# Weight slices at eight places in SBUF, and another order of the contraction in the second feed-forward

## The chip, the cores and the metric

The kernel runs on one NeuronCore of a Trainium2 chip. The metric is the device time of one launch in microseconds. The kernel before takes 2028.67 us, the median of three runs (2028.02 to 2029.2).

## The reference

One inference step of a one-layer decoder on 288 positions: 256 of a prompt and 8 x 4 of samples that are being decoded. D_MODEL is 2048, D_FF is 5632, and everything is float32.

```python
def rms_norm(x, g):
    ...
def swiglu(x, w_gate, w_up, w_down):
    return (jax.nn.silu(x @ w_gate) * (x @ w_up)) @ w_down

def decoder_layer(x, lp, h0, k_past, v_past):
    x = x + 0.5 * swiglu(rms_norm(x, lp['ffn1_norm']), lp['ffn1_w_gate'], lp['ffn1_w_up'], lp['ffn1_w_down'])
    hn = rms_norm(x, lp['mix_norm'])
    z = hn @ lp['w_in']
    u, q, k, v = jnp.split(z, ...)
    y_ssm, h_last = s5_mixer(u, h0, ...)            # state space scan over the positions
    ...                                             # norms of q and k, keys of the cache
    y_attn = window_attention(q, kk, vv, ...)       # window of 128 positions
    merged = jnp.concatenate([rms_norm(y_ssm, lp['ssm_out_norm']), rms_norm(y_attn, lp['attn_out_norm'])], axis=-1)
    x = x + merged @ lp['w_out']
    x = x + 0.5 * swiglu(rms_norm(x, lp['ffn2_norm']), lp['ffn2_w_gate'], lp['ffn2_w_up'], lp['ffn2_w_down'])
    return x, k_state, v_state, h_last
```

The positions are columns here: the residual x is kept as 16 tiles of 128 features x 288 positions, and every projection has a weight block as the stationary operand and a tile of activations as the moving one.

## The kernel before

**Pieces and splits.** All weights are read once, in 680 pieces of 128 x 1024, 128 x 768 or 128 x 640 float32: gate and up projections, down projections, then w_in and w_out in the mixing stage, then the second feed-forward. The class `Weights` brings them in. `load` (line 75) issues a piece's DMA from SP into a tile `raw`, of which there are five. `split` (line 83) makes two tiles of it for TensorE's fp32r format: `wh`, the rounded weights (a cast on ACT, line 88), and `wl`, what the rounding lost (a subtraction on DVE, line 89). Of `wh` and of `wl` there are three each. `next` (line 103) hands the present piece to TensorE, splits up to two pieces ahead and loads up to five ahead. It also runs other work that is bound to the number of a piece. So each engine's order is written out by hand, and each queue is strictly in that order.

**Matmuls.** Activations are split the same way, into `xh` and `xl` (or `hh` and `hl` for what goes into a down projection). A piece holds eight slices of 128 columns (six or five in a down projection). For each slice k `mm3` issues three matmuls into one PSUM bank, lines 272 to 274: `wh` with the high tile, `wh` with the low tile, `wl` with the high tile. Each streams 128 x 288 and has its own weight load of 128 x 128.

**Places.** A moving tile of 288 float32 takes 1,152 bytes of a partition, four and a half times 256, so the next tile starts 128 bytes beside it, modulo 256. Between the 16 tiles `xh` and the 16 tiles `xl` lies a tile of 32 float32, `gap_x`, that serves nothing else; `gap_r` and `gap_y` do the same for `hh` and `hl`. So the moving operands of a slice's three matmuls, and of neighbouring slices, start in turn 128 bytes beside a multiple of 256 and on one. `gap_w`, 56 float32 ahead of the weight tiles, makes `raw`, `wh` and `wl` start on multiples of 256, and with 512 bytes to a slice every slice does.

**Stages.** The first feed-forward takes pieces 0 to 303, in four rounds of eleven gate and up units and a down projection of 16 x 2 pieces each. The small tables of the state space part are made beside it, and a few transposes on TensorE come between its pieces. The mixing stage takes pieces 304 to 375, and the second feed-forward 376 to 679.

Of the kernel before, what the change touches and what calls it, by code (L numbers as in the profile page):

```python
# [10 lines left out]
F32 = mybir.dt.float32  # L11
F32R = mybir.dt.float32r
# [5 lines left out]
P = 128  # L18
# [7 lines left out]
N = T * W1  # L26
# [4 lines left out]
HALF = 8 * P  # L31
# [15 lines left out]
class Weights:  # L47
# [28 lines left out]
    def load(self):  # L76
        ap = self.pieces[self.nl]
        n = ap.shape[-1]
        t = self.pool.tile([P, HALF], F32, name="raw", bufs=5)
        self.nc.sync.dma_start(t[:, :n], ap)  # L80
        self.raw[self.nl] = (t, n)
        self.nl += 1

    def split(self):
        t, n = self.raw.pop(self.ns)
        wh = self.pool.tile([P, HALF], F32R, name="wh", bufs=3)
        wl = self.pool.tile([P, HALF], F32R, name="wl", bufs=3)
        self.nc.scalar.copy(wh[:, :n], t[:, :n])  # L88
        self.nc.vector.tensor_tensor(wl[:, :n], t[:, :n], wh[:, :n].bitcast(F32), op=ALU.subtract)  # L89
        self.hl[self.ns] = (wh, wl)  # L90
        self.ns += 1
# [25 lines left out]
def tile_hymba_step(ctx, tc, io):  # L117
# [14 lines left out]
    def ffn_units(l):  # L132
        seq = []
        for c in range(NCK):
            for f in range(CH):
                if not (c > 0 and f == 0):
                    seq.append(("gu", c * CH + f))
            if c + 1 < NCK:
                seq.append(("gu", (c + 1) * CH))
            seq.append(("down", c))  # L140
        return seq
# [27 lines left out]
    xh = [cp.tile([P, N], F32R, name="xh%d" % k) for k in range(KT)]  # L169
    cp.tile([P, 32], F32, name="gap_x")  # L170
    xl = [cp.tile([P, N], F32R, name="xl%d" % k) for k in range(KT)]
# [96 lines left out]
    def mm3(ps, wh, wl, kts, rh, rl, first, last):  # L268
        n = len(kts)
        for a, k in enumerate(kts):  # L270
            s = slice(a * P, (a + 1) * P)
            pe.matmul(ps, wh[:, s], rh[k], start=first and a == 0, stop=False)  # L272
            pe.matmul(ps, wh[:, s], rl[k], start=False, stop=False)  # L273
            pe.matmul(ps, wl[:, s], rh[k], start=False, stop=last and a == n - 1)  # L274

    def projs(n):

        ps = [pm.tile([P, 512], F32, name="main") for _ in range(n)]
        for hf in range(2):
            for p_ in ps:  # L280
                wh, wl = W.next()
                mm3(p_[:, :N], wh, wl, range(8 * hf, 8 * hf + 8), xh, xl, hf == 0, hf == 1)
        return ps

    def proj():
        return projs(1)[0]

    def ffn(l, post, hp, first):
        HH, HL = {}, {}
        hold = Hold(W.i + first)  # L290
        early = [] if l else projs(3)

        def gate(f, pg, s2):
            t1 = tp.tile([P, N], F32, name="t1")
            s1 = tp.tile([P, N], F32, name="s1")
            dve.tensor_tensor(t1, pg[:, :N], R, op=ALU.mult)  # L296
            act.activation(s1, t1, AF.Silu)  # L297
            pool_e.tensor_tensor(s2, s1, R, op=ALU.mult)  # L298

        def up(f, pu, s2):  # L300
            h = tp.tile([P, N], F32, name="h")
            hh = hp.tile([P, N], F32R, name="hh")
            if f == 0:
                hp.tile([P, 32], F32, name="gap_r", bufs=1)
            hl = hp.tile([P, N], F32R, name="hl")
            dve.tensor_tensor(h, pu[:, :N], s2, op=ALU.mult)  # L306
            act.copy(hh, h)  # L307
            dve.tensor_tensor(hl, h, hh.bitcast(F32), op=ALU.subtract)  # L308
            HH[f % CH, f // CH], HL[f % CH, f // CH] = hh, hl

        def gu(f):
            s2 = tp.tile([P, N], F32, name="s2")
            pg = early.pop(0) if early else proj()
            hold(lambda: gate(f, pg, s2))
            pu = early.pop(0) if early else proj()
            hold(lambda: up(f, pu, s2))

        def down(c):
            rh = {k: HH.pop((k, c)) for k in range(CH)}
            rl = {k: HL.pop((k, c)) for k in range(CH)}  # L320
            for d in range(KT):
                ps = pm.tile([P, 512], F32, name="main")
                wh, wl = W.next()
                mm3(ps[:, :N], wh, wl, range(6), rh, rl, True, False)
                wh, wl = W.next()
                mm3(ps[:, :N], wh, wl, range(6, CH), rh, rl, False, True)
                dve.scalar_tensor_tensor(x[d], ps[:, :N], 0.5, x[d], op0=ALU.mult, op1=ALU.add)  # L327
                if c == NCK - 1:
                    post(d)

        for kind, j in ffn_units(l):
            (gu if kind == "gu" else down)(j)
# [275 lines left out]
    with ExitStack() as es:  # L608
        mix(tc, nc, io, es, W, MIX0, dict(
            x=x, xh=xh, xl=xl, gains=gains, ident=ident, ones=ones, acc=acc, R=R, tp=tp,  # L610
            dr=dr, pm=pm, pa=pa, proj=proj, mm3=mm3, norm=norm, rsqrt=rsqrt, now=now, Hold=Hold,
            mats=mats, e4=e4, h4=h4, h0=h0, post=post_norm(32)))
# [646 lines left out]
```

## Time and profile before

| | |
|---|---|
| median of three runs | 2028.67 us |
| profiled execution, its own time | 2031.1 us |
| span from first to last instruction | 2029.3 us |
| mean granted TensorE clock | 0.997 |
| TensorE matmuls, share of the span | 99% (15,248) |
| DVE, ACT, POOL | 60%, 42%, 15% |
| moved by DMA | 359.04 MB, 177 GB/s |

Busy time of TensorE counts from a matmul's start to its modelled end, and matmuls overlap in it. It tells that the engine had work, not how fast the work went. That is read from how many matmuls start in a stretch. PEld is the engine's weight load, which runs beside the matmuls.

### The profile page before, as it was taken

The page shows a single profiled execution, that of the slowest core. Times are in us where ns is not written, and L with a number is a line of the kernel's source. Part 1 is how long each engine was busy: PE and PEld are TensorE (multiplying, and loading weights), DVE is VectorE, ACT ScalarE, POOL GpSimd, SP SyncE. Part 2 cuts the span into 40 slices and gives each one's busy share as a digit, 9 for nine tenths or more (in the row PEclk, how much of TensorE's full clock was granted, in tenths as well). Part 3 has the DMA queues.
Part 4 walks back from the last instruction along what each step waited for, and adds up shares of the span by engine and source line. Part 5 has one row for each costly group of instructions (what it writes and reads, how often), then busy time and mean ns, then how long its engine had stood idle before and what let it go on. Part 6 is the DMA issues. An engine that isn't in the chain of part 4 may idle for free. (4 is left out here: it accounts for less than half of the span.)

```text
span 2029.3 us, 37632 instructions
## 1 busy us (share of the span) xinstructions
PE 2008.7 (99%) x15248; PEld 1995.9 (98%) x15248; DVE 1212.0 (60%) x1873; ACT 851.5 (42%) x1334; POOL 295.8 (15%) x451
## 2 busy tenths in 40 slices
PE   8999999999999999999999999999999999999999
PEld 7999999999999999999989999999999999999999
DVE  5577666666656645686787874455444544454444
ACT  5433443444444434533476543333333333333332
POOL 3110011001110000212367730000000000000000
PEclk9999999999999999999999999999999999999999
DMA  6555645565656565678634445556555655465554
GB/s 225 194 164 148 210 158 203 173 208 162 203 172 196 176 197 151 216 235 276 221 120 136 151 162 166 164 144 190 161 164 147 185 165 163 147 181 168 166 159 148
DMA packets 122622, 359.04 MB, mean 177 GB/s; under 512 B 22448, under 2 KB 30256, under 8 KB 121264
## 3 DMA queue, kind: packets, MB, share of 16 engines
q1 hardware_dynamic: 114672, 340.81, 53.4%
q10 hardware_dynamic: 7776, 15.83, 2.3%
q8 instruction: 119, 1.95, 0.4%
q14 instruction: 55, 0.45, 0.1%
HBM read 338.40 MB, written 20.22 MB: 177 GB/s over the span
## 5 line engine op out<-in xcount | busy, mean ns | idle before, releaser
L89 DVE TENSOR_TENSOR wl<-raw,wh 128x1024 fp32r<-128x1024 f32 (+2 forms) x680 | 760.2, 1118 | 540.0 <-ACT wh L88 538.1
L272 PE MATMUL main<-xh,wh 128*128 128x288 f32 x3136 | 932.6, 297 | 6.1 <-ACT xh L180 6.1
L273 PE MATMUL main<-xl,wh 128*128 128x288 f32 x3136 | 927.4, 296 | 1.3 <-DVE xl L181 1.3
L274 PE MATMUL main<-xh,wl 128*128 128x288 f32 x3136 | 927.5, 296 | 0.9 <-DVE wl L89 0.7
L88 ACT CAST wh<-raw 128x1024 fp32r<-128x1024 f32 (+2 forms) x680 | 643.5, 947 | 626.8 <-PE main L273 413.1
L272 PEld LDWEIGHTS main<-xh,wh 128*128 128x128 f32 x3136 | 593.6, 189 | 7.1 <-ACT xh L180 6.1
L273 PEld LDWEIGHTS main<-xl,wh 128*128 128x128 f32 x3136 | 593.6, 189 | 2.4 <-DVE xl L181 2.1
L274 PEld LDWEIGHTS main<-xh,wl 128*128 128x128 f32 x3136 | 593.4, 189 | 1.3 <-DVE wl L89 1.3
L272 PE MATMUL main<-hh,wh 128*128 128x288 f32 x1664 | 494.1, 297 | 0.0
L273 PE MATMUL main<-hl,wh 128*128 128x288 f32 x1664 | 491.1, 295 | 0.3 <-DVE hl L674 0.3
L274 PE MATMUL main<-hh,wl 128*128 128x288 f32 x1664 | 490.6, 295 | 0.0
L273 PEld LDWEIGHTS main<-hl,wh 128*128 128x128 f32 x1664 | 313.8, 189 | 0.7 <-DVE hl L674 0.5
L274 PEld LDWEIGHTS main<-hh,wl 128*128 128x128 f32 x1664 | 313.7, 189 | 0.0
L272 PEld LDWEIGHTS main<-hh,wh 128*128 128x128 f32 x1664 | 313.2, 188 | 0.4
L298 POOL TENSOR_TENSOR s<-s,R 128x288 f32<-128x288 f32 x88 | 71.2, 809 | 1255.2 <-ACT s L297 1255.2
L297 ACT ACTIVATE s<-t 128x288 f32<-128x288 f32 x88 | 39.1, 445 | 238.3 <-DVE t L296 238.3
L307 ACT CAST hh<-h 128x288 fp32r<-128x288 f32 x88 | 38.1, 433 | 240.1 <-DVE h L306 240.1
L327 DVE SCALAR_TENSOR_TENSOR x<-main,x 128x288 f32<-128x288 f32 x128 | 58.4, 456 | 50.9 <-PE main L274 49.0
L306 DVE TENSOR_TENSOR h<-main,s 128x288 f32<-128x288 f32 x88 | 40.2, 457 | 77.3 <-PE main L274 77.1
L296 DVE TENSOR_TENSOR t<-main,R 128x288 f32<-128x288 f32 x88 | 40.2, 457 | 64.5 <-PE main L274 64.0
L308 DVE TENSOR_TENSOR hl<-h,hh 128x288 fp32r<-128x288 f32 x88 | 40.3, 458 | 44.0 <-ACT hh L307 44.0
L190 POOL TENSOR_TENSOR acc<-acc,sq 128x288 f32<-128x288 f32 x45 | 48.9, 1086 | 56.5 <-ACT sq L186 55.2
(263 smaller groups left out, 877.9 us busy)
## 6 DMA issues: line engine op xcount, KB each, us to landing
raw<-in_w_gu SPq DMA_DIRECT2D x352, 512.0 KB, 3.5
raw<-in_w_dn SPq DMA_DIRECT2D x128, 384.0 KB, 3.1
raw<-in_w_dn SPq DMA_DIRECT2D x128, 320.0 KB, 2.9
raw<-in_w_in SPq DMA_DIRECT2D x40, 512.0 KB, 4.1
raw<-in_w_out SPq DMA_DIRECT2D x32, 512.0 KB, 3.4
mats<-stage ACTq DMA_DIRECT2D x8, 1536.0 KB, 7.0
mb<-mats SPq DMA_DIRECT2D x8, 768.0 KB, 5.1
ma<-mats SPq DMA_DIRECT2D x8, 512.0 KB, 4.2
```

The costliest lines, as they stand in the source:

```text
L88: self.nc.scalar.copy(wh[:, :n], t[:, :n])
L89: self.nc.vector.tensor_tensor(wl[:, :n], t[:, :n], wh[:, :n].bitcast(F32), op=ALU.subtract)
L190: eng.tensor_tensor(acc, acc, sq, op=ALU.add)
L272: pe.matmul(ps, wh[:, s], rh[k], start=first and a == 0, stop=False)
L273: pe.matmul(ps, wh[:, s], rl[k], start=False, stop=False)
L274: pe.matmul(ps, wl[:, s], rh[k], start=False, stop=last and a == n - 1)
L296: dve.tensor_tensor(t1, pg[:, :N], R, op=ALU.mult)
L297: act.activation(s1, t1, AF.Silu)
L298: pool_e.tensor_tensor(s2, s1, R, op=ALU.mult)
L306: dve.tensor_tensor(h, pu[:, :N], s2, op=ALU.mult)
L308: dve.tensor_tensor(hl, h, hh.bitcast(F32), op=ALU.subtract)
L327: dve.scalar_tensor_tensor(x[d], ps[:, :N], 0.5, x[d], op0=ALU.mult, op1=ALU.add)
```

## The change

It has three parts. `wh` and `wl` become tiles of 1,088 columns, of which 1,024 are used, from column o on. o is 0 for the first eight pieces, 8 for the next eight, and so on to 56, and then 0 again: 0, 32, 64 ... 224 bytes beside a multiple of 256. There are four `raw` tiles in place of five. And in the gate and up projections of the second feed-forward (l = 1, so step = 2) the eight slices of a piece are taken in the order 0 2 4 6 1 3 5 7. A slice keeps its columns in the piece, b in `mm3`.

```diff
     def load(self):
...
-        t = self.pool.tile([P, HALF], F32, name="raw", bufs=5)
+        t = self.pool.tile([P, HALF], F32, name="raw", bufs=4)
...
     def split(self):
         t, n = self.raw.pop(self.ns)
-        wh = self.pool.tile([P, HALF], F32R, name="wh", bufs=3)
-        wl = self.pool.tile([P, HALF], F32R, name="wl", bufs=3)
+        o = 8 * (self.ns // 8 % 8)
+        wh = self.pool.tile([P, HALF + 64], F32R, name="wh", bufs=3)[:, o:o + HALF]
+        wl = self.pool.tile([P, HALF + 64], F32R, name="wl", bufs=3)[:, o:o + HALF]
...
         for a, k in enumerate(kts):
-            s = slice(a * P, (a + 1) * P)
+            b = k - kts[0]
+            s = slice(b * P, (b + 1) * P)
...
-    def projs(n):
+    def projs(n, step=1):
...
-                mm3(p_[:, :N], wh, wl, range(8 * hf, 8 * hf + 8), xh, xl, hf == 0, hf == 1)
+                ks = [8 * hf + a for b in range(step) for a in range(b, 8, step)]
+                mm3(p_[:, :N], wh, wl, ks, xh, xl, hf == 0, hf == 1)
...
-    def proj():
-        return projs(1)[0]
+    def proj(step=1):
+        return projs(1, step)[0]
...
-            pg = early.pop(0) if early else proj()
+            pg = early.pop(0) if early else proj(1 + l)
...
-            pu = early.pop(0) if early else proj()
+            pu = early.pop(0) if early else proj(1 + l)
```

The number and the kinds of instructions on every engine are the same, and no row on ACT, DVE, POOL or SP changes its place. Lines move down by one to three (`mm3`'s are 274 to 276 after). The places in SBUF of all tiles but `raw`, `wh` and `wl` are the same modulo 512. In the built program 3,744 of the 14,400 matmuls of `mm3` have weights 0 or 128 bytes beside a multiple of 256, and 10,656 have them at one of the six other places.

TensorE's order changes in the second feed-forward alone. Its first gate piece begins so before; xh_87 to xh_94 are the high tiles of slices 0 to 7, xl_104 to xl_111 the low ones, and even slices have their high tile 128 bytes beside a multiple of 256 and their low tile on one:

```order
8265 L272 MATMUL main<-xh_87,wh 128x288
8266 L273 MATMUL main<-xl_104,wh 128x288
8267 L274 MATMUL main<-xh_87,wl 128x288
8268 L272 MATMUL main<-xh_88,wh 128x288
8269 L273 MATMUL main<-xl_105,wh 128x288
8270 L274 MATMUL main<-xh_88,wl 128x288
8271 L272 MATMUL main<-xh_89,wh 128x288
```

And after, in the same place:

```order
8265 L274 MATMUL main<-xh_87,wh 128x288
8266 L275 MATMUL main<-xl_104,wh 128x288
8267 L276 MATMUL main<-xh_87,wl 128x288
8268 L274 MATMUL main<-xh_89,wh 128x288
8269 L275 MATMUL main<-xl_106,wh 128x288
8270 L276 MATMUL main<-xh_89,wl 128x288
8271 L274 MATMUL main<-xh_91,wh 128x288
```

Slice 0 is followed by slice 2, so two high tiles of even slices stand next to each other (rows 8267 and 8268) where a high tile of an odd slice stood.

The end of that piece and the begin of the next on TensorE, before; xh_95 is the first high tile of the second half of the features:

```order
8283 L272 MATMUL main<-xh_93,wh 128x288
8284 L273 MATMUL main<-xl_110,wh 128x288
8285 L274 MATMUL main<-xh_93,wl 128x288
8286 L272 MATMUL main<-xh_94,wh 128x288
8287 L273 MATMUL main<-xl_111,wh 128x288
8288 L274 MATMUL main<-xh_94,wl 128x288
8289 L272 MATMUL main<-xh_95,wh 128x288
```

And after:

```order
8283 L274 MATMUL main<-xh_92,wh 128x288
8284 L275 MATMUL main<-xl_109,wh 128x288
8285 L276 MATMUL main<-xh_92,wl 128x288
8286 L274 MATMUL main<-xh_94,wh 128x288
8287 L275 MATMUL main<-xl_111,wh 128x288
8288 L276 MATMUL main<-xh_94,wl 128x288
8289 L274 MATMUL main<-xh_95,wh 128x288
```

The piece ends with slices 5 and 7, whose neighbours are again of one class (rows 8285 and 8286), and the step to the next piece, from slice 7 to slice 8, is as before.

## The prediction

> **What bounds the kernel now.** I read the page first: its busy shares, and the shares of the chain that ended last.
>
> ```profile
> PE 2008.7 (99%) x15248; PEld 1995.9 (98%) x15248; DVE 1212.0 (60%) x1873; ACT 851.5 (42%) x1334; POOL 295.8 (15%) x451
> PEclk9999999999999999999999999999999999999999
> PE 41%; DVE 0%; issue 0%
> PE main L272 14%; PE main L274 14%; PE main L273 14%; PE main L206 0%; DVE x L327 0%
> ```
>
> TensorE is busy in 99% of the span at full clock, and the chain, as far back as it is followed (41% of the span), is nothing but the three matmul lines. So the end is set by how far apart the matmuls start. There are 14,400 of them in these lines (3 x 3136 + 3 x 1664), and 1 ns more in each spacing is 14.4 us of the kernel. The duration that a group shows for one matmul (some 296 ns) is of no use here, since two or three are drawn over each other; the spacing has to be counted. The next view does that: the busy time of TensorE in chosen stretches, with the count x of matmuls. Each is drawn 0.29 us long, so about two of a count were already running when the stretch opened; I leave those two off.
>
> ```profile
> core 0: us, PE busy (x), PEclk, DMA share, GB/s
> 46.00:168.00 122.00, 122.00 (x917) 1.00 0.52 168
> 294.00:355.00 61.00, 61.00 (x471) 1.00 0.56 189
> 370.00:382.00 12.00, 12.00 (x94) 1.00 0.41 112
> 495.00:556.00 61.00, 61.00 (x472) 1.00 0.59 190
> 571.00:598.00 27.00, 27.00 (x210) 1.00 0.56 185
> 695.00:794.00 99.00, 99.00 (x764) 1.00 0.54 174
> 1192.00:1335.00 143.00, 143.00 (x1075) 1.00 0.50 159
> 1547.00:1616.00 69.00, 69.00 (x522) 1.00 0.59 174
> ...
> 913.20:916.30 3.10, 3.10 (x15) 0.50 1.03 425
> ```
>
> The reader is to see three speeds of the same instruction at the same clock. From 46 to 168 us it is 122/915 = 133.3 ns, and from 1192 to 1335 us 143/1073 = 133.3. From 294 to 355 us it is 61/469 = 130.1, and from 695 to 794 us 99/762 = 129.9. In a down projection (1547 to 1616 us) it is 69/520 = 132.7. The last row is a stretch in which half the clock was granted: 3.10/13 = 238 ns, so one matmul alone needs about 119 ns at full clock. The other 11 to 14 ns are not its own streaming. The timeline of a 130 ns stretch shows what they are tied to:
>
> ```profile
> 320.07 0.29 PE L274 MATMUL main<-xh,wl 128*128 128x288 f32 x1
> 320.07 0.19 PEld L272 LDWEIGHTS main<-xh,wh 128*128 128x128 f32 x1
> 320.20 0.29 PE L272 MATMUL main<-xh,wh 128*128 128x288 f32 x1
> 320.20 0.19 PEld L273 LDWEIGHTS main<-xl,wh 128*128 128x128 f32 x1
> 320.33 0.29 PE L273 MATMUL main<-xl,wh 128*128 128x288 f32 x1
> ```
>
> The load for the next matmul starts when a matmul starts, and the next matmul follows 0.13 us later, although streaming takes only 0.12. So I read the spacing as the time of a weight load. The chain of waits in a 133.3 ns stretch gives each spacing as the length of a piece:
>
> ```profile
> 1190.82 0.14 PE main L274
> 1190.96 0.13 PE main L272
> 1191.09 0.13 PE main L273
> 1191.22 0.13 PE main L274
> 1191.36 0.14 PE main L272
> ...
> 1191.89 0.14 PE main L273
> ```
>
> One spacing in four is long: 0.14 us, at 1190.82, 1191.36 and 1191.89. With three at 131 the fourth is 4 x 133.3 - 3 x 131 = 140 ns. A tile that is streamed has 1,152 bytes, four and a half times 256, and by the gap of 128 bytes between the high and the low tiles each matmul's operand lies 128 bytes away, modulo 256, from the operand before it. Four steps keep the class, so the long spacing always falls on the same one of the two classes. By the addresses in the built program it is the class that lies 128 bytes beside a multiple of 256; the other starts on the multiple, as every weight slice does. So equal matmuls differ by where operand and weights stand to each other, and half of the shifted class pays. In the 130 ns stretches nobody pays.
>
> **The change part by part.** *Places of the weights.* Nothing is added on any engine: the same 680 ACT casts and 680 DVE subtractions write the same sizes, and the 14,400 matmuls read the same sizes. What changes is the first byte. Counted in the built program, 3,744 matmuls get slices 0 or 128 bytes beside a multiple of 256, and 10,656 get 32, 64, 96, 160, 192 or 224. At 0 nothing changes; 128 only swaps which class of operand is the shifted one, and I price both at nothing. For the other six places there is no row, since no stretch has them. Bounds from the nearest rows: not under the 130.0 of the fast stretches, not over the 140 of the long spacing. What do they pay now? The five fast stretches are 260 us, or 2,000 matmuls; 4,224 are in the down projections at 132.7; 8,176 remain at 133.3. The mean is 132.7. So the bounds are (130.0 - 132.7) x 10,656 = -29 us and (140 - 132.7) x 10,656 = +78 us. Between them I take 134.4. At these six places both classes of operand stand off the weights, as only one does now. If each class pays as the shifted class pays today, the spacing is the mean of 140 and 131, 135.5. If a paid collision also spares the next three matmuls, whichever class they are, it stays 133.3, and only the fast stretches are lost. 134.4 lies half way. That is 1.7 x 10,656 = +18 us.
>
> *Order 0 2 4 6 1 3 5 7.* It adds no instruction. In 176 pieces of the second feed-forward (4,224 matmuls, at 133.3 now) operands of one class meet six times in a piece (the third matmul of one slice and the first of the next). Before, such a meeting is found only in the down projections, once in 33 matmuls (eleven slices), and there the mean is 132.7: a meeting is worth 33 x 0.6 = 20 ns. Six of them cannot bring a piece under 130.0, so the gain is at most 3.3 x 4,224 = 14 us. The loss is bounded by the half of a piece in which two matmuls in three are of the shifted class: (2 x 135.5 + 131)/3 = 134.0, or 0.7 x 4,224 = +3 us. Only a quarter of these pieces keep a place at which I know the pattern, so I take a quarter of 14: -4 us.
>
> *Four raw buffers for five.* The load five pieces ahead now waits for the split of the piece one ahead, not of the present one: one piece later, 3.2 us (24 x 133 ns). Queued behind it on SP are the other loads of the mixing stage, and the matmuls there wait for those.
>
> ```profile
> raw<-in_w_gu SPq DMA_DIRECT2D x352, 512.0 KB, 3.5
> raw<-in_w_dn SPq DMA_DIRECT2D x128, 384.0 KB, 3.1
> SPq L80 <- DVE wl L89: 1402.7, 577, 7.3
> ACT wh L88 <- PE main L273: 413.1, 272, 6.7
> ACT wh L88 <- DMA raw<-in_w_gu: 5.4, 4, 2.5
> 865.00:1136.00 271.00, 263.44 (x2135) 0.99 0.60 192
> ```
>
> SP already waits 577 times for a split, and ACT, which splits, waits for TensorE 272 times but for a landing 4 times, 5.4 us in all. A raw piece has about four pieces' time from its issue to its use, 8.8 us where pieces are shortest (16.5 matmuls, 2.2 us each), against 3.1 us to land and some 2 for the splits. That cover hides the later issue. If it is gone, each late landing holds TensorE. The one stretch with idle time on TensorE, the mixing stage, has 271 - 263.4 = 7.6 us of it; I bound the cost by as much again, +8, and below by 0, since a later issue lets nothing start earlier. I take +1.
>
> *The sum.* This execution took 2031.1 us, 2029.3 of it the span. 2031.1 + 18 - 4 + 1 = 2046. The median of the runs is 2028.67, 2.4 below it, so I forecast 2044, with 2033 to 2062 as this case's own range (133.3 to 135.5 elsewhere). Under 0.2%, 4 us, a measurement cannot tell from no change.
>
> **The rivals.** *The other places are fast* (other side). A collision then needs slice and operand exactly 128 bytes apart, and at six of eight places every matmul runs at 130.0 as from 695 to 794 us. That is -29 - 4, or 1996. The point that decides is a mean of 132.7 at the new places. For it: the fast stretches show that 130.0 is held for 99 us. Against it: it is the weaker pattern, 2,000 matmuls of 14,400, and from 1192 to 1335 us, between the same operands, it is not met.
>
> *Weights' place is indifferent*, and the long spacing comes from something else. Then only the order is left, 2025 to 2029. The Trainium skill says this: TensorE: Matmul & The Clock Gate, section "Step-by-step: what each phase is for", has two independent read ports, so that loading the next weights takes nothing from the running matmul. SBUF — State Buffer, section "Who interferes with whom", has TensorE never waiting on anyone. Against this rival stands 133.3 beside 130.0 at clock 1.00, with one class of operand marked; for it, that the trace never shows another place of the weights, so the cause may sit in the operand's place alone.
>
> *Every load at a 32-byte place is long.* If slices at 32, 96, 160 and 224 (7,104 matmuls) need more reads, each spacing is 140: 7.3 x 7,104 = +52, about 2078 with the rest as forecast or better; all six places would give 2107.
>
> *Late loads.* If landings in the mixing stage come late one after the other, TensorE waits in that stage twice as long as now: +8 in place of +1, and about 2051. It decides where a landing takes over four pieces' time.
>
> **How the numbers follow.** The chances go by how much of the trace each has on its side. Forecast 0.43; fast places 0.26; indifferent 0.13; long loads 0.14; late loads 0.04. Faster is 0.26 and a third of the indifferent, 0.30. No change is the rest of it and 0.05 from the forecast's lower edge, 0.14. Slower is 0.56. The range 1999 to 2084 leaves out the faster part of the fast places and the worse part of the long loads, about 0.1 each. Cases of both signs hold the chance, so the forecast's own range above is the narrower statement.
>
> **What the profile after would show.** Groups of eight pieces are 25 us long, so stretches cut at their bounds give the spacing of each place: 133.3 or less at 0 and 128, 133.3 to 135.5 at the others if I am right; 130.0 there makes me wrong, and so does 140 in every second group. In the second feed-forward the groups at 0 and 128 should show less than 133.3. ACT should still wait for landings some 5 us in all, and the mixing stage should keep its 7.6 us of idle TensorE. What I can least exclude is that a step of the place every 25 us itself throws the matmuls from one pattern into the other.

## The result, and the profile after

The changed kernel takes 2039.26 us, the median of four runs (2038.23 to 2042.96), against 2028.35 for the kernel before: a ratio of 1.0057, 95% interval 1.004 to 1.0075, 11 us slower. The profiled execution of after took 2038.27 us, its span 2036.5, 7.2 more than the span before. The two profiled executions lie closer together than the medians: that of before, 2031.1 us, is longer than the four timed ones (2027.44 to 2029.2), that of after is among the shorter of its four.

Lines of the page of after, on busy shares, clock and the chain that ended last:

```profile
PE 2011.7 (99%) x15248; PEld 1998.6 (98%) x15248; DVE 1213.6 (60%) x1873; ACT 852.3 (42%) x1334; POOL 295.8 (15%) x451
PEclk9999999999999999999999999999999999999999
PE 41%; DVE 0%; issue 0%
```

Nothing here tells the two kernels apart: TensorE is busy in 99% of the span at full clock, as before. The difference is in how far apart the matmuls start, and in one stage. The busy time of TensorE in the three stages, first feed-forward, mixing stage, second feed-forward, before (cut at the first matmul of the next stage):

```profile
0.00:864.70 864.70, 855.26 (x6435) 1.00 0.58 186
864.70:1181.40 316.70, 309.14 (x2478) 0.99 0.58 188
1181.40:2029.30 847.90, 844.26 (x6339) 1.00 0.53 163
```

And after:

```profile
0.00:871.00 871.00, 860.70 (x6435) 1.00 0.57 184
871.00:1190.80 319.80, 308.98 (x2479) 0.99 0.59 187
1190.80:2036.50 845.70, 841.98 (x6339) 1.00 0.53 165
```

The same matmuls take 6.3 us more in the first feed-forward, 3.1 more in the mixing stage, and 2.2 less in the second feed-forward. The sum is the 7.2 us.

Now the groups of eight pieces that the prediction wanted to see: stretches of after that begin and end with a group, 192 matmuls each (x shows two or three more, which were running when the stretch opened). The first six lie in the first feed-forward, with weights at 64, 96, 192, 224, 0 and 32; the last four in the second, at 0, 32, 64 and 96:

```profile
65.77:91.15 25.38, 25.38 (x194) 1.00 0.53 178
91.15:116.75 25.60, 25.60 (x194) 1.00 0.61 214
698.69:724.08 25.39, 25.39 (x194) 1.00 0.64 224
724.08:749.68 25.60, 25.60 (x195) 1.00 0.51 165
749.68:775.26 25.58, 25.58 (x194) 1.00 0.51 165
775.26:800.85 25.59, 25.59 (x194) 1.00 0.46 137
1217.36:1242.96 25.60, 25.60 (x195) 1.00 0.57 182
1242.96:1268.46 25.50, 25.50 (x195) 1.00 0.52 165
1268.46:1293.84 25.38, 25.38 (x194) 1.00 0.51 167
1293.84:1319.23 25.39, 25.39 (x194) 1.00 0.52 166
```

25.38/192 is 132.2 ns, 25.50 is 132.8, 25.59 is 133.3. In the old order (first six) 64 and 192 give 132.2, and 0, 32, 96 and 224 give 133.3. In the new order (last four) 0 is still 133.3, 32 is 132.8, 64 is 132.2 and 96 is 132.2. No stretch is at 130.0. The group at 0 from 749.68 us lies where before, from 691.65 to 794.47 us, the weights were at 0 too and matmuls started 130.0 ns apart.

For all of a kind I also took each spacing, from one matmul's start to the next one's, from the trace, and put the place of the weights beside it. Over the 14,400 matmuls (spacings of 115 to 150 ns, so without the gaps where other work stands between) the mean is 132.55 before and 132.85 after. By place, all stages and both orders together, it is 133.03 at 0, 133.16 at 32, 132.21 at 64, 132.92 at 96, and the same within 0.13 at 128, 160, 192 and 224: it repeats every 128 bytes. Gate and up matmuls of the first feed-forward went from 131.51 to 133.03 (x 4,224 = 6.4 us), those of the second from 133.32 to 132.70 (2.6 us less), which is what the stages show.

### The profile page after: what moved, and what is told of

Read it like the earlier page. It is cut to its first block, busy times and chain, and to the rows that moved or that the text cites. A ratio compares the mean times of both kernels' runs of the same rounds, so it can differ in the third digit from the quotient of the medians.

```text
span 2036.5 us, 37629 instructions
## 1 busy us (share of the span) xinstructions
PE 2011.7 (99%) x15248; PEld 1998.6 (98%) x15248; DVE 1213.6 (60%) x1873; ACT 852.3 (42%) x1334; POOL 295.8 (15%) x451
```

## The experiments

Ratios are against the kernel before, timed beside each run. "Means" are those of the spacings as above. An edit is shown against the kernel before where nothing else is said, and "..." marks code that is left out.

### The three parts, one at a time

Places alone (with four raw buffers, which they need for room), the old order, shown against the changed kernel:

```diff
-            pg = early.pop(0) if early else proj(1 + l)
+            pg = early.pop(0) if early else proj()
...
-            pu = early.pop(0) if early else proj(1 + l)
+            pu = early.pop(0) if early else proj()
```

> The eight places and four raw buffers, without the new order. Theory A (the place sets the spacing, and only relative to the moving tiles modulo 128): gate and up pieces of the second feed-forward go from the 132.7 ns that the changed kernel shows there to the 133.0 that the first feed-forward shows at the same places, 4,224 x 0.3 = +1 us, so 2040 to 2041, +0.6% over before. Theory B (the order is what costs, the places are nothing): the time falls back to 2028 to 2030.

Measured: 1.0037 (1.0024 to 1.005). The groups of the second feed-forward, at 0, 32, 64 and 96, now in the old order:

```profile
1217.66:1243.25 25.59, 25.59 (x195) 1.00 0.57 181
1243.25:1268.84 25.59, 25.59 (x195) 1.00 0.50 165
1268.84:1294.23 25.39, 25.39 (x195) 1.00 0.52 167
1294.23:1319.83 25.60, 25.60 (x195) 1.00 0.50 165
```

Places alone give a slowdown. Beside after's rows these also show what the order does at each place: nothing at 0 and at 64, 0.5 ns less at 32, 1.1 ns less at 96.

The order alone, weights at 0, five raw buffers, again against the changed kernel:

```diff
-        t = self.pool.tile([P, HALF], F32, name="raw", bufs=4)
+        t = self.pool.tile([P, HALF], F32, name="raw", bufs=5)
...
-        o = 8 * (self.ns // 8 % 8)
-        wh = self.pool.tile([P, HALF + 64], F32R, name="wh", bufs=3)[:, o:o + HALF]
+        wh = self.pool.tile([P, HALF], F32R, name="wh", bufs=3)
```

> The new order alone: five raw buffers, all weights on multiples of 256. Theory A: in the changed kernel the pieces at place 0 have 133.33 ns in the new order and the kernel before has 133.32 in the old one, so nothing, 2027 to 2030. The prediction's term: six meetings of one class in a piece save a quarter of 14 us or more, 2015 to 2025. Theory B: the order costs the 11 us, 2038 to 2041.

Measured: 1.0003 (0.9994 to 1.0013). The second run of gate and up pieces of the second feed-forward, eleven units, 1,056 matmuls:

```profile
1404.57:1545.36 140.79, 140.79 (x1059) 1.00 0.51 161
```

140.79/1,056 is 133.3, as before. At 0 the order changes how often a spacing is long (137 ns or more: 17% in place of 25%), but the others grow by as much, and the mean does not move.

Four raw buffers alone:

```diff
-        t = self.pool.tile([P, HALF], F32, name="raw", bufs=5)
+        t = self.pool.tile([P, HALF], F32, name="raw", bufs=4)
```

> Four raw buffers alone. Theory A: nothing in the spacings; at most the 2.6 us by which the spacings over 150 ns have grown in the changed kernel, 2028 to 2031, and the stretches at 130.0 ns in the first feed-forward are still there. Theory C (late loads make the kernel slower, not the places): 2035 to 2041, with TensorE idle in the mixing stage.

Measured: 1.0013 (1.0003 to 1.0023), 2.6 us. The mean spacing is 132.57, as before. The cost is in the mixing stage, which takes 321.1 us in place of 316.7. TensorE's wait for the scan's input U, before, in after and in this kernel (us in total, times, longest):

```profile
PE main L723 <- DMA U<-ud: 2.4, 2, 1.3
```

```profile
PE main L726 <- DMA U<-ud: 5.7, 3, 3.3
```

```profile
PE main L723 <- DMA U<-ud: 4.7, 3, 2.6
```

The five kernels with four raw buffers have 4.7 to 5.7 us here, the nine with five 1.0 to 3.0. Loads of U stand on SP behind loads of raw pieces, and those now wait for a buffer one piece longer: counted from the first matmul of the mixing stage, the 32 loads of U start at 58.2 us in the mean before, and at 62.0 in this kernel.

### Which distance counts

All weights at 64, four raw buffers, old order (the line is shown against the changed kernel):

```diff
-        o = 8 * (self.ns // 8 % 8)
+        o = 16
```

> All weights 64 bytes beside a multiple of 256, old order, four raw buffers. Theory A: every piece has the 132.2 ns that the changed kernel shows at 64 and 192, no spacing of 0.14 us, no stretch at 130.0: 14,065 x (132.2 - 132.55) = -5 us, 2023 to 2026 with up to 2.6 us for the buffers. Theory D (it is the step of the place every eight pieces that disturbs, not the place): a fixed place brings the stretches at 130.0 back, and the time is 2028 or below 2015, as these stretches are as long as before or longer.

Measured: 0.9984 (0.9975 to 0.9994), although the four buffers cost 2.6 us. Two runs of gate and up pieces, 791 matmuls in the first feed-forward (where the kernel before has 130.0) and 1,056 in the second (where it has 133.3), first in the kernel before, then in this one:

```profile
691.54:794.37 102.83, 102.83 (x793) 1.00 0.55 175
1407.00:1547.80 140.80, 140.80 (x1059) 1.00 0.52 161
```

```profile
692.43:797.01 104.58, 104.58 (x794) 1.00 0.53 175
1411.92:1551.54 139.62, 139.62 (x1059) 1.00 0.50 163
```

104.58/791 and 139.62/1,056 are both 132.2. At 64 there is one pattern, without long spacings, and all the stages have it.

Then the weights stay at 0 and the streamed tiles move by 64, with five raw buffers:

```diff
+    cp.tile([P, 16], F32, name="gap_m")
     xh = [cp.tile([P, N], F32R, name="xh%d" % k) for k in range(KT)]
...
-    cp.tile([P, 56], F32, name="gap_w")
+    cp.tile([P, 40], F32, name="gap_w")
```

> The kernel before with its weights where they were and the tiles that are streamed in the feed-forwards (xh and xl) 64 bytes further on; nothing else moves. If the distance of weights and streamed operand modulo 128 decides, gate and up matmuls start 132.2 ns apart in both feed-forwards, without long spacings and without any stretch at 130.0: the first feed-forward loses 0.8 ns x 4,224 = 3 us and the second gains 1.1 x 4,224 = 4.6 us, so 0.998 to 1.000 of the time before. If the place of the weights by itself decides, the gate and up matmuls stay as before, 131.5 and 133.3 with the stretches at 130.0, and the ratio is 1.000.

Measured: 0.9992 (0.9983 to 1.0002), and the same two runs:

```profile
692.26:796.84 104.58, 104.58 (x793) 1.00 0.53 172
1408.20:1547.82 139.62, 139.62 (x1058) 1.00 0.52 162
```

To the hundredth of a microsecond what weights at 64 gave, with the weights where they were. The down projections, whose operands did not move, stayed at 132.7 in the mean. So it is the distance between the weights and the streamed operand that sets the spacing, modulo 128 bytes, and not the place of the weights alone. (The streamed operands alternate by 128 bytes, so a distance of 0 is here always 0 and 128 in turn.) The rival that the place of the weights is indifferent falls. The Trainium skill, TensorE: Matmul & The Clock Gate, section "Step-by-step: what each phase is for", has loading and streaming on two independent read ports, so that loading the next weights takes nothing from a running matmul. The trace does not agree for these operands: 132.2 against 133.3 by 64 bytes of distance.

All weights at 128, four raw buffers, old order (again against the changed kernel):

```diff
-        o = 8 * (self.ns // 8 % 8)
+        o = 32
```

> Four raw tiles, the old order, all weights 128 bytes beside a multiple of 256. If only the distance modulo 128 counts, this is the kernel with four raw tiles alone: 1.001, the same stretches at 130.0 behind the transposes, gate and up at 131.5 in the first feed-forward and 133.3 in the second. If the class of the operand counts on which TensorE starts behind the transposes, 128 exchanges the classes, the stretches at 130.0 are gone and both are near 133.3: 1.8 x 4,224 = 7.6 us more, 1.005. If it was the steps between places that threw the matmuls out of the 130 ns pattern, a fixed place keeps it: 1.001 again.

Measured: 1.0057 (1.004 to 1.0074). The same two runs, and the first of them with four raw buffers and weights at 0:

```profile
695.99:801.44 105.45, 105.45 (x794) 1.00 0.54 173
1419.81:1560.60 140.79, 140.79 (x1059) 1.00 0.51 162
```

```profile
688.90:791.72 102.82, 102.82 (x793) 1.00 0.54 177
```

105.45/791 is 133.3; at 0 it is 130.0. With a fixed place nothing steps, and the 130 ns stretches are gone all the same. Weights at 128 exchange the two classes of operand, and TensorE starts behind the transposes on the class that lay at distance 128 before and lies at 0 now. So the stretches at 130.0 seem to hang on the way in which a run is begun. That gave the question of the next runs: can such a beginning be made?

### How a 130 ns stretch is begun

In the kernel before, each such stretch begins behind the same work, the last product for a table of the state space part (two float32 matmuls with 256 columns in one bank). A feed-forward has four runs of gate and up pieces, of 12, 11, 11 and 10 units, each with a down projection behind it. Eight single float32 matmuls of 256 columns that nothing reads, near the start of these runs:

```diff
+        def kick():
+            ps = pa.tile([P, 512], F32, name="main")
+            pe.matmul(ps[:, :256], ones, x[0][:, :256], start=True, stop=True)
...
+            if f in (12, 23, 34) or f == 4 * (1 - l):
+                W.at(W.i + 1, kick)
```

> The kernel before with eight more matmuls of float32, 128 x 256, that nothing reads, one at the start of each run of gate and up pieces, ahead of a second half. If the way in which a run is begun decides between 130.0 and 133.3 at one and the same place, gate and up of the second feed-forward go from 133.3 to 130.0 (3.3 x 4,224 = 14 us less) and those of the first from 131.5 towards 130.0 (some 4 us less), against 8 x 0.4 us that the new matmuls take: 2013 to 2016, 0.993. If the stretches at 130.0 need the transposes themselves, or idle memory, nothing changes but the 3 us: 1.0015.

Measured: 1.0021 (1.0006 to 1.0036). None began a stretch at 130.0. The part of a second feed-forward run behind one of them, 1,031 matmuls, is at 133.3:

```profile
1412.28:1549.74 137.46, 137.46 (x1034) 1.00 0.51 159
```

The same with the weights of the down projections at 64, shown against the run above:

```diff
         t, n = self.raw.pop(self.ns)
...
+        o = 16 if n < HALF else 0
+        wh, wl = wh[:, o:o + n], wl[:, o:o + n]
```

> The same with the weights of the down projections 64 bytes beside a multiple of 256 (their pieces are shorter than the tile, so no tile grows). If places add up as the other runs had them, down projections go from 132.7 to 132.2, 0.5 x 4,224 = 2 us less than with the eight matmuls alone: 2011 to 2014, 0.992. If a change of place between the runs spoils the pattern that the eight matmuls start, the gain of those is gone and 1.000 is left.

Measured: 0.9987 (0.9977 to 0.9996). Down projections went from 132.70 to 132.21 in the mean, as expected. One run, the second of the first feed-forward, was at 130.0, and was so from its first matmuls, ahead of the extra one: it came so out of the down projection. Nor did the extra one end it: behind it the spacings were 322, 126 and again 130 in the mean. The ratio is some 3 us better than the spacings account for, which stays open.

Then the streamed rows of the eight matmuls at other places, shown against the first run of this part:

```diff
-            pe.matmul(ps[:, :256], ones, x[0][:, :256], start=True, stop=True)
+            pe.matmul(ps[:, :256], ones, x[0][:, o:o + 256], start=True, stop=True)
```

> As the run with eight more matmuls of float32, but what these stream lies at other places: 64 bytes (modulo 128) from the weights that come next in the runs that begin at gate and up unit 4 and 23 of the first feed-forward and 2 of the second, a multiple of 256 (0) in those from unit 12 and 34 of the first and 12 of the second, 96 bytes in the run from unit 23 of the second and 32 in the one from unit 34. Before, the streamed rows lay at 128 and the first spacings behind were 325 and 132 ns; behind the transposes' last product, whose streamed rows start at 64, they are 322 and 126 and the 130 ns pattern follows. If the distance between that last stream and the next weights decides, the runs with 64 show 321 and 126 and then 130.0, those with 0 as well if a distance of 0 is also free, and 96 and 32 tell which of them are: four of the runs at 130.0 would be some 10 us less, 0.996. If the transposes' other parts decide, all stay at 133.3 and the ratio is 1.002.

Measured: 1.002 (1.0011 to 1.003). No run turned; behind each the first spacings were 324 or 325 and 132 or 133 ns, whatever the place. The distance of the extra matmul's own stream is not what decides.

Then 36 kinds of extra work in one kernel, each in a gate and up unit of its own, ahead of the second half of the gate piece:

```diff
+                if hf and kk:
+                    kick(*kk, wh)
```

> The kernel before with one extra bit of TensorE work, that nothing reads, in 36 of the 44 gate and up units of the second feed-forward, another one each time, always ahead of the second half of the gate piece: a float32 matmul of 32 to 280 columns, two of 256 into one bank, one and two of 256 columns in four stretches of 64 (the form of the transposes' last product), one to three transposes, and matmuls in the weights' own format of 64 to 272 columns, on a tile of the one or the other class. Each unit then tells whether what follows it starts 133.3 or 130.0 ns apart. If the phase in which the first weight load meets the stream decides, some of the 36 give 130.0, those whose first spacing is 126 or less, and the mean of the second feed-forward's gate and up falls below 133.3 by the share of such units. If the pattern needs what lies around the transposes, all stay at 133.3. The extra work costs 0.1 to 1 us each, some 15 us together; the time is of no interest here.

Measured: 2037.6 us in one execution, beside 2032.41 of the kernel before. Seven of the 36 gave 130.0 in the matmuls behind them: two float32 matmuls of 256 columns, two transposes, and matmuls in the weights' own format with 64, 128 and 192 columns on a high tile, and 96 and 160 on a low one. Behind these seven the first gap was followed by a spacing of 125 or 126 ns, and behind the 29 others by 130 or more. The stretches behind 64, 96, 128 and 160 columns on a high tile, each from its extra matmul to the next one, with 96 matmuls of the kernel in it:

```profile
1626.75:1639.35 12.60, 12.60 (x100) 1.00 0.52 174
1639.35:1652.24 12.89, 12.89 (x99) 1.00 0.50 164
1652.24:1664.84 12.60, 12.60 (x100) 1.00 0.50 169
1664.84:1677.72 12.88, 12.88 (x99) 1.00 0.48 164
```

12.60 is 96 x 130.0 and 0.12 for the extra matmul; 12.89 is 96 x 133.3 and 0.09. The columns are not the whole reason: 96 and 160 met TensorE in the 130 ns pattern and threw it out. All six extra works that came in such a stretch in this kernel did. What those six would do in a 133.3 ns stretch was not tried.

### A version that beats both

The shortest of the seven, 64 columns, once in each run:

```diff
+    RUNS = (4, 12, 23, 34), (2, 12, 23, 34)
...
+                if hf and kick:
+                    pe.matmul(pa.tile([P, 512], F32, name="main")[:, :64], wh[:, :P], xh[8][:, :64],
+                              start=True, stop=True)
...
+            pg = early.pop(0) if early else proj(f in RUNS[l])
```

> The kernel before with eight short matmuls in the weights' own format, 128 x 64, that nothing reads, one ahead of the second half of a gate piece near the start of each run of gate and up pieces (first feed-forward units 4, 12, 23 and 34, second 2, 12, 23 and 34). In the scan such a one turned 133.3 into 130.0 for the 72 matmuls up to the next extra work, with a first spacing of 126 ns, and took some 115 ns. If the pattern, once begun, holds as long as nothing else comes between, some 3,900 gate and up matmuls of the second feed-forward go from 133.3 to 130.0 (13 us less) and some 1,400 of the first (4.5 us less): 2028.35 - 17 + 1 = 2012, 0.9915 to 0.993. If it holds only for some pieces, or the start depends on the state that the run before left, a part of that: 0.995 to 0.999, and the windows tell which runs missed.

Measured: 2021.36 us, 0.9947 (0.9928 to 0.9966). The timeline at the start of the second run of the second feed-forward (start and drawn length in us):

```profile
1403.32 0.29 PE L274 MATMUL main<-xh,wl 128*128 128x288 f32 x1
1403.45 0.20 PE L285 MATMUL main<-xh,wh 128*128 128x64 f32 x1
1403.49 0.38 PE L272 MATMUL main<-xh,wh 128*128 128x288 f32 x1
1403.70 0.29 PE L273 MATMUL main<-xl,wh 128*128 128x288 f32 x1
1403.83 0.29 PE L274 MATMUL main<-xh,wl 128*128 128x288 f32 x1
```

The extra matmul starts in its turn at 1403.45, and the next one already at 1403.49; the one after it waits until 1403.70. So the whole costs 0.38 us for what takes 0.26 without it. Two of the four runs of the second feed-forward behind their extra matmul, which turned, and the two others:

```profile
1403.70:1537.73 134.03, 134.03 (x1033) 1.00 0.52 162
1611.37:1745.40 134.03, 134.03 (x1033) 1.00 0.52 163
1205.58:1330.23 124.65, 124.65 (x937) 1.00 0.50 158
1818.78:1943.42 124.64, 124.64 (x936) 1.00 0.52 159
```

134.03/1,031 is 130.0, held for 134 us; 124.65/935 is 133.3. All four runs of the first feed-forward turned. In the two that missed, the last long spacing belonged to the second matmul ahead of the extra one, in the six that turned to the fourth. The gain follows from the means: (131.51 - 130.47) x 4,224 + (133.32 - 131.68) x 4,224 = 11.3 us, less 8 x 0.11, is 10.4 us, and the ratio says 10.8.

With the down projections at 64 too, and without the extra matmul in unit 12 of the first feed-forward, shown against the run above:

```diff
+        o = 16 if n < HALF else 0
+        wh, wl = wh[:, o:o + n], wl[:, o:o + n]
...
-    RUNS = (4, 12, 23, 34), (2, 12, 23, 34)
+    RUNS = (4, 23, 34), (2, 12, 23, 34)
```

> The same with the weights of the down projections 64 bytes beside a multiple of 256, and without the short matmul at unit 12 of the first feed-forward, where the earlier run with places at 64 had 130 ns without help. Down projections go from 132.7 to 132.2, 2 us less than the run beside it: 0.9905 to 0.992. If the place of the down projections sets another state at the start of the runs behind them, some runs stay at 133.3, each 3 to 4 us of the gain: 0.993 to 0.997.

Measured: 2020.93 us, 0.9941 (0.9922 to 0.996). A gate and up run, the down projection behind it (528 matmuls), and the last gate and up run:

```profile
1408.90:1542.93 134.03, 134.03 (x1033) 1.00 0.53 163
1542.93:1612.74 69.81, 69.81 (x531) 1.00 0.60 174
1823.37:1948.03 124.66, 124.66 (x937) 1.00 0.51 158
```

69.81/528 is 132.2 in place of 132.7. But the last run came out of its down projection at 130.0 by itself this time, and the extra matmul threw it out to 133.3; the run at unit 12 of the first feed-forward, left without one, was at 133.3. So the gain of the place comes on top, but the starts do not stay where they were. The two versions cannot be told apart, and both beat the kernel before and the changed one.

## Why the prediction was right, and where it was not

It forecast slower, 2044 us, within 2033 to 2062; it is 2039.26. The direction came from the right place, TensorE's spacings, and the size of the terms was off in both directions. By the spacings the places cost 5.5 us (places alone against four raw buffers alone) and the order saves 1.5; with some 3 for the buffers that is 7 us, the difference of the two profiled spans. The medians say 11, with 8 to 15 in the interval, and the 4 us between are not explained. That the forecast of +15 lies so near is in part luck: its largest term is five times too large, and what it lacked elsewhere makes up some of that.

**Other places, +18 us.** Places alone against four raw buffers alone is 1.0037/1.0013, some 5 us, and 7.2 us by their two spans. Of the 5.5 us by their spacings 3.6 fall at the six other places: 0.34 ns for each of the 10,656 matmuls in place of the 1.7 in the sum. The term was mis-sized: "134.4" was taken half way between 135.5, each class of operand paying as the shifted one, and 133.3, "a paid collision also spares the next three matmuls, whichever class they are". The lower number is right for 32, 96, 160 and 224 (133.3 in gate and up, in the old order). Its reason fits 32 and 160, where one spacing in four is long as before; at 96 and 224 hardly any is, and the number came out right by luck. At 64 and 192 it is less than either, 132.2, a value that no row before showed. What the prediction had as its lower case, that "only the fast stretches are lost", is what the loss is: 6.4 us of gate and up in the first feed-forward.

**Places 0 and 128, nothing.** Wrong: 1.9 of the 5.5 us fall there, all in the first feed-forward. "At 0 nothing changes" overlooked that a stretch at 130.0 has to be begun while the weights are at 0, and that it ends where they leave 0. Of the eight table products of after one meets weights at 0, for one piece of 15 matmuls, and behind it these start 129 and 131 ns apart in turn, until the place steps to 32. All gate and up groups at 0 that TensorE came to from another place were at 133.3. And 128 is not 0 with the classes exchanged: at a fixed 128 the same table products begin nothing. What the prediction could "least exclude", that steps of the place throw the matmuls from one pattern into the other, is so for the way into a group; but the fixed 128 shows that the loss needs no step.

**The order, -4 us.** By itself it is nothing (1.0003), and in after it saves 1.4 us in the second feed-forward (847.1 without it, 845.7 with it), none of that at 0 or 128, where the prediction expected it and said that the groups should show less than 133.3. The step that failed is "a meeting is worth 20 ns", taken from the down projections: at distances of 0 and 128 six meetings in a piece leave the mean where it was. What makes the 132.7 of the down projections is not shown. The gain came at 32, 96, 160 and 224, at which the prediction claimed none.

**Four raw buffers, +1 us.** It is 2.6 us by the ratio, and 3.1 us longer in the mixing stage of after, inside the bound of 8. The mechanism was named (loads of the mixing stage queued behind on SP, TensorE waiting for those), and the cover that was trusted, four pieces' time, covers nearly all pieces but not the loads of U behind them. ACT's waits for landings, which should have stayed at 5 us, became 13.8:

```profile
ACT wh L89 <- DMA raw<-in_w_dn: 7.1, 3, 2.5
ACT wh L89 <- DMA raw<-in_w_gu: 6.7, 4, 2.6
```

The 7.6 us of idle TensorE in that stage, which should have stayed, became 319.80 - 308.98 = 10.8.

**The rivals.** Fast places at 130.0 did not come; the nearest is 132.2 at two of the six. Every load long at 32-byte places did not come either: at 32 one in four is long, and at 96 and 224 hardly any is, with the same mean. Late loads came, above all for U, at 3 us and not 8.

What stays open is what in the memory or in TensorE makes the distance count modulo 128 bytes, and what fixes which of the two patterns a start leads to. Only the distance of 64 was made in both ways; for the others the weights alone were moved.

## What to carry to other kernels

Where weight loads and matmuls run beside each other at full clock and TensorE is busy throughout, count the starts in stretches of a hundred microseconds: a busy share of 99% hid 130.0, 132.2 and 133.3 ns for the same instruction. Vary the distance between the weights and the streamed operand modulo 128 bytes (64 was even and never long here), and treat a faster pattern as a state that has to be begun and can be lost: one extra matmul of 64 columns in each run was worth 10.8 us, though two of the eight began nothing. A buffer given up to make room was paid here by what stands behind its loads in the queue, hardly by the loads themselves.

## What the runs showed of the hardware

- Matmuls of 128 x 288 in this format, in gate and up pieces in slice order, start 130.0, 132.2 or 133.3 ns apart at one granted clock (1.00 in all these rows), by the distance between weights and operand modulo 128 bytes and, where the operands lie at 0 and 128 in turn, by the way in which the run began.
- With all weights at 64 there is one pattern whatever the start: 132.21 to 132.23 in every stage, for up to 6,286 spacings without other work between.
- A pattern at 130.0, once begun, was held for 1,031 matmuls and 134 us. Each of the six extra works that came into one in the scan ended it, and one float32 matmul of 256 columns in another run did not.
- Start times repeat: the same 791 matmuls took 104.58 us in two different kernels at distance 64, and 102.82 to 102.83 in those at 0.
